# New order of projection tiles and new lane paces in a fused mLSTM + S5 decoder block

## The chip, the cores and the metric

The kernel runs on one core of a Trainium2 chip. The metric is the device time of one execution in microseconds, the median of several. The core has a matrix engine (PE in the profile, its weight loads PEld), a vector engine (DVE), a scalar engine (ACT), GpSimd (POOL) and a queue engine that here only issues transfers (SP). Each works through its own list of instructions; semaphores tie them together.

## What is computed

One decoder block over 16 meta and 1024 real positions, width 1024, all in float32:

```
p     = h @ w_in + b_in            columns [u_s5 | q | k | v | o | i | f | g_s5 | g_m]
y_s5  = GLU(GELU(S5(u_s5)))        S5: diagonal complex recurrence, 32 groups of 16
y_m   = (o * HeadNorm(mLSTM(q, k, v, i, f))) @ m_w_out     4 heads, chunkwise
mix   = sigmoid(g_s5) * y_s5 + sigmoid(g_m) * y_m
h     = LN(alpha * h + mix @ w_o)
h     = LN(alpha * h + relu(h @ w_up + b_up)^2 @ w_down)
```

q and k pass a causal convolution of width 4 and a SiLU first. GLU(z) is the first half of `z @ w_glu` times the sigmoid of the second.

## The kernel before

**Arithmetic.** Each float32 operand of a large product is split into a high part (a copy to float32r by ACT, `whi`, `hT_hi`, `gelh`) and the remainder (a subtraction by DVE, `wlo`, `hT_lo`, `gell`). A product is three matmuls, lines 226 to 228 in `mm3`. So each weight tile costs one transfer (SP, line 198, tile `wraw`), one ACT copy (line 212) and one DVE subtraction (line 213) before PE can use it. `split_w` gives the split a higher scheduling priority; a job's weights are split while the job ahead of it runs, and loaded while the one or two ahead of that run.

**Jobs.** After the first layer norm (`ln0_pipe`, up to about 75 us) the projections run as a list of jobs, in the order of the string `ORDER`. A `q` entry makes two jobs, q and k of a head. `v` jobs make the values of a head, `u` jobs the inputs of S5, `o` jobs the output gate of half a head, `g` jobs the S5 gate (8 tiles), `m` jobs two of the 8 tiles of the gate g_m. Behind them come eight GLU jobs, z0 to z7, then the rest of g_m and the output product (`first`, `run7`, with sums of weights formed by POOL transfers in `w_sums`), then the output projection and the feed-forward part.

**Lanes.** The recurrences are generators in queues called lanes. `ml` holds the gate computation and the four heads of the mLSTM one after another, `cv` the convolutions, `s5c` the tables and constants of S5, `s5` its four batches, `s5g` the GELU, `ah` the scaling of the residual and the early preparation of up-projection weights (`up_early`). After every two terms of a product `mm3` calls `pump`, which adds the planned time of these matmuls to a clock and lets each lane take its next step if its last `yield` is over:

```
def pump(dt):
    clock[0] += dt
    for l in lanes.values():
        l.run(clock[0])
```

With 512 columns dt is 1.28. A step is emitted at the first such call after it is due. The numbers in the lists `ML`, `NL`, `C5`, `K5`, `D5`, `W5`, `Y5` are the yields, by head or by S5 batch. A head of `mlstm` first loads its decay rows from DRAM, forms them by DVE and ACT (lines 440 to 452; yields 6.0, nine of 0.3, 4.0), and then walks over 9 chunks with two yields of ML[h] each, with a norm of four chunks (`N`) after chunk 5 and at the end. Then the two tiles of the head are ready for its `o` jobs.

Two places don't pace. Ahead of an `o` job the `ml` lane is stepped at once until its head is ready, and at z0 the S5 lanes are drained. What is emitted is then ordered for each engine by the framework's scheduler, with the order of emission as priority.

**Memory.** 30 slots of 128 x 1056 floats (`big`) hold weights, lanes, S5 tiles, gates and GELU outputs. Before, the 8 S5 gate tiles `SG` and the 8 GELU tiles `GEL` (high and low of 4 batches) stay in slots from where they are made until the GLU jobs use them; z_f takes `SG[f]` over as `MIX[f]`.

**Queues.** SP issues nearly all transfers: weights, the S5 round trips through DRAM (us_dr, cs_dr, ct_dr, ys_dr), hm_dr (line 913, an o job's result), act_dr. POOL issues w_sums (line 995) and the small transfers of S5's constants.

Of the kernel before, what the change touches and what calls it, by code (L numbers as in the profile page):

```python
# [9 lines left out]
F32 = mybir.dt.float32  # L10
F32R = mybir.dt.float32r
# [26 lines left out]
LN2_1 = 0.693359375  # L38
LN2_2 = math.log(2.0) - LN2_1
MAGIC = 1.5 * 2 ** 23  # L40
ORDER = "q0 q1 v0 q2 v1 q3 o1 o0 v2 o2 o3 u0 u1 v3 u2 g0 u3 g1 o4 o5 o7 o6 g2 g3 g5 g6 g4 g7 m0 m1"
S5_START = "v0"
NM = 2
SPLIT_UP = 200
PRE = 3
ZD = 1
ML = [2.4, 1.2, 1.68, 4.8]
NL = [0.88, 1.75, 1.75, 1.75]
C5 = [1.9, 1.9, 1.9, 1.9]
K5 = [1.7, 1.7, 1.7, 1.7]  # L50
Z5 = [1.0, 1.0, 1.0, 1.0]
D5 = [2.88, 1.22, 1.44, 1.44]
W5 = [2.21, 1.56, 2.6, 2.6]
Y5 = [1.97, 2.82, 3.38, 2.82]
AFT = 0
VAFT = 2
LOAD0 = "x0 x1 w0 c0 x2 w1 c1 x3 x4 w2 x5 w3 x6"
# [55 lines left out]
def decoder_block(  # L113
# [4 lines left out]
    nc = tc.nc  # L118
    v_, a_, g_, t_ = nc.vector, nc.scalar, nc.gpsimd, nc.tensor
# [9 lines left out]
    def slot(name, dt=F32):  # L129
        return big.tile([P, SLOT], dt, tag="s", name=name)  # L130
# [7 lines left out]
    def f32(ap):  # L138
        return ap.bitcast(F32)
# [1 line left out]
    def row_bcast(src, n, off=0):  # L141
        return bass.AP(tensor=src.tensor, offset=src.offset + off, ap=[[0, P], [1, n]])

    lanes = {"ml": Lane(), "cv": Lane(), "s5": Lane(), "s5c": Lane(), "s5g": Lane(), "ah": Lane()}
    clock = [0.0]

    def pump(dt):
# [131 lines left out]
    QK, VT, HM, HMREADY = {}, {}, {}, set()  # L279
# [31 lines left out]
    def v_job(h):  # L311
        W = 264 if h == 0 else 256
        if h == 0:
            loads = [(wv0[:, 4 * i:4 * i + 4].rearrange("p k f -> p (k f)"), 4 * W) for i in range(2)]
        else:
            loads = [(wv[h - 1, :, 4 * i:4 * i + 4].rearrange("p k f -> p (k f)"), 4 * W) for i in range(2)]

        def run(job):
            bvt = mid.tile([P, DV], F32, tag="bvt", bufs=1, name="bvt")
            nc.sync.dma_start(bvt, row_bcast(bv, DV, h * DV))  # L320
            if h == 0:
                v_.memset(IF[:, 0, 0, :], NEG)
                v_.memset(IF[:, 1, 0, :], 100.0)
            v0 = mid.tile([P, 258], F32, tag="v0", bufs=2, name="v0")
            v12 = [slot("v12"), slot("v12")]
            vt = [v0] + [v12[i // 4][:, (i % 4) * 258:(i % 4) * 258 + 258] for i in range(8)]
            VT[h] = vt
            for i in range(NCH):
                c0, n = chunk(i)
                ps = mmps()  # L330
                terms = []
                for k in range(KT):
                    wh, wl = job.w[k // 4]
                    s = slice((k % 4) * W, (k % 4) * W + W)
                    terms.append((hT_hi[:, k, c0:c0 + n], hT_lo[:, k, c0:c0 + n], wh[:, s], wl[:, s]))
                g_.memset(vt[i][:n, DV:DV + 1], 1.0)
                if i == 0:
                    for k in range(KT):
                        _, _, wh, wl = terms[k]
                        t_.matmul(ps[:48, :W], meta_hl[:, k, :], wh, start=(k == 0), stop=(k == KT - 1))  # L340
                    p2 = mmps()
                    for k in range(KT):
                        _, _, wh, wl = terms[k]
                        t_.matmul(p2[:n, :W], meta_hl[:, k, :n], wl, start=(k == 0), stop=(k == KT - 1))
# [13 lines left out]
                if i == VAFT:
                    job.after()
            if h == 0:  # L360
                lanes["ml"].add(gates())
            lanes["ml"].add(mlstm(h))
        all_jobs.append(Job(loads, run))

# [64 lines left out]
                          bass.AP(tensor=src.tensor, offset=src.offset + (4 + h) * P,  # L429
                                  ap=[[0, P], [4 * P, NCH - 1], [1, P]]))  # L430

    def mlstm(h):
        while (h, 1) not in QK:
            yield 0.5
        qT, kT, vt = QK[h, 0], QK[h, 1], VT[h]
        gB, wiB = slot("gB"), slot("wiB")
        bcast_row(gB, grow_dr, h)
        bcast_row(wiB, wrow_dr, h)
# [232 lines left out]
    GEL = {}  # L671
# [4 lines left out]
    def s5_tables():  # L676
        lo, hi, tmp = ([slot("s5T"), slot("s5T")] for _ in range(3))
        c1, s1 = (t[:, :1040].rearrange("p (q c) -> p q c", q=16) for t in lo)
        c2, s2 = (t[:, :1040].rearrange("p (q c) -> p q c", q=16) for t in hi)
        g_.memset(c1[:, :, 0], 1.0)  # L680
        g_.memset(s1[:, :, 0], 0.0)
        g_.tensor_copy(c1[:, :, 1], S5["p8"][:, 0])
        g_.tensor_copy(s1[:, :, 1], S5["p8"][:, 1])
        yield 1.9

        def product(oc, os, n, m, ac, as_, bc, bs):
            w1, w2 = (t[:, 0:16 * m].rearrange("p (q c) -> p q c", q=16) for t in tmp)
            sh = [P, 16, m]
            cmul(v_, oc, os, ac, as_, bc.to_broadcast(sh), bs.to_broadcast(sh), w1, w2)
        n = 1  # L690
        while n < 64:
            product(c1[:, :, n + 1:2 * n + 1], s1[:, :, n + 1:2 * n + 1], n, n, c1[:, :, 1:n + 1], s1[:, :, 1:n + 1],
                    c1[:, :, n:n + 1], s1[:, :, n:n + 1])
            n *= 2
            yield 1.9
        product(c2[:, :, 0:64], s2[:, :, 0:64], 64, 64, c1[:, :, 1:65], s1[:, :, 1:65], c1[:, :, 64:65], s1[:, :, 64:65])
        yield 3.8
        product(c2[:, :, 64:65], s2[:, :, 64:65], 128, 1, c1[:, :, 1:2], s1[:, :, 1:2], c2[:, :, 63:64], s2[:, :, 63:64])
        for r in range(2):
# [187 lines left out]
    def s5_gelu(b):  # L887
        yield 3.0
        yc = slot("s5yc")
        for g in range(8):  # L890
            src = ys_dr[b, :, (g % 2) * 4 + g // 2, :].rearrange("(t h) c -> h t c", h=16)
            nc.sync.dma_start(yc[16 * g:16 * g + 16, 0:1024].rearrange("p (t c) -> p t c", t=8), src)
        yield 14.0
        gf = slot("gelf")
        a_.activation(gf[:, 0:1024].rearrange("p (c t) -> p t c", t=8),
                      yc[:, 0:1024].rearrange("p (t c) -> p t c", t=8), AF.Gelu_apprx_tanh)
        hi, lo = slot("gelh", F32R), slot("gell", F32R)
        a_.activation(hi[:, 0:1024], gf[:, 0:1024], AF.Copy)
# [21 lines left out]
        return hi, lo  # L920

    MIX, SG, SGM = {}, {}, {}

    def gs_job(f):
        def evac(bi, c0, c1, ps):
            if bi == 0:
                SG[f] = slot("sgs")
            a_.activation(SG[f][:, c0:c1], ps, AF.Sigmoid, bias=bft[:, JGS + f:JGS + f + 1])
        fm_job(JGS + f, HALF, META, evac)

    def glu_job(f):
        def run(job):
# [560 lines left out]
    for i, j in enumerate(jobs):  # L1493
# [612 lines left out]
```

## Time and profile before

| | us |
|---|---|
| median of 3 runs | 1594.03 (1590.19 to 1595.22) |
| the profiled execution | 1587.66 |
| its span, from the first to the last instruction | 1585.9 |
| mean granted PE clock | 0.981 |

The stages, by the profile: the first norm with the first projections until 75 us; projections, mLSTM, S5 and GLU until about 720 us, with gates and output product behind; feed-forward from about 980 us on. In the views below, a waits row reads "engine line waited for: total, times, longest"; a row of a timeline reads "start, length, engine, line, operation, tiles, shape, [idle before, and what ended it]"; a row of lines reads "line, engine, operation, tiles, count | busy, mean ns | idle before"; a row of transfers reads "tiles, queue, count, KB each, us to landing".

### The profile page before, as it was taken

The page shows a single profiled execution, that of the slowest core. Times are in us where ns is not written, and L with a number is a line of the kernel's source. Part 1 is how long each engine was busy: PE and PEld are TensorE (multiplying, and loading weights), DVE is VectorE, ACT ScalarE, POOL GpSimd, SP SyncE. Part 2 cuts the span into 40 slices and gives each one's busy share as a digit, 9 for nine tenths or more (in the row PEclk, how much of TensorE's full clock was granted, in tenths as well). Part 3 has the DMA queues.
Part 4 walks back from the last instruction along what each step waited for, and adds up shares of the span by engine and source line. Part 5 has one row for each costly group of instructions (what it writes and reads, how often), then busy time and mean ns, then how long its engine had stood idle before and what let it go on. Part 6 is the DMA issues. An engine that isn't in the chain of part 4 may idle for free.

```text
span 1585.9 us, 20447 instructions
## 1 busy us (share of the span) xinstructions
PE 1521.4 (96%) x7593; PEld 1282.3 (81%) x7593; DVE 1059.3 (67%) x1939; ACT 642.0 (40%) x982; POOL 93.5 (6%) x183
## 2 busy tenths in 40 slices
PE   7998989999897999999999999999999999999997
PEld 7997969899776878777788888888888888888886
DVE  7797766445556234468779666766666769775876
ACT  5623444533344231235545224544444534432440
POOL 0010413200000011000000001000000000000000
PEclk9998999999998999999999999999999999999999
DMA  8527433464562565677335226744444699666642
GB/s 297 166 48 119 125 98 119 148 181 152 159 157 71 140 197 197 219 280 255 128 126 180 81 80 208 256 140 151 148 154 145 198 362 336 233 219 237 227 171 107
DMA packets 150308, 278.15 MB, mean 175 GB/s; under 512 B 39472, under 2 KB 61688, under 8 KB 150152
## 3 DMA queue, kind: packets, MB, share of 16 engines
q1 hardware_dynamic: 124144, 249.84, 47.1%
q0 software_dynamic: 26064, 27.01, 7.1%
q8 instruction: 59, 0.97, 0.2%
q14 instruction: 41, 0.34, 0.1%
HBM read 197.21 MB, written 92.97 MB: 183 GB/s over the span
## 4 chain that ended last, share of the span: by engine, by line
PE 39%; issue 15%; DMA 1%; DVE 0%; SPq 0%; ACT 0%; POOLq 0%
PE mm L228 9%; PE mm L227 9%; PE mm L226 9%; PE sd L226 3%; PE sd L227 3%; PE sd L228 3%; DMA rawb<-h_dr 1%; PE ln L1593 0%; DMA wraw<-in_wf_dram 0%; DVE wlo L1064 0%; DVE rawb L1023 0%; SPq L1045 0%; POOLq L2102 0%; ACT whi L1063 0%; ACT hT_hi L1018 0%
## 5 line engine op out<-in xcount | busy, mean ns | idle before, releaser
L226 PE MATMUL mm<-hT_hi,whi 128*128 128x512 f32 (+3 forms) x604 | 228.1, 378 | 3.7 <-ACT whi L212 3.7
L228 PE MATMUL mm<-hT_hi,wlo 128*128 128x512 f32 (+3 forms) x604 | 226.9, 380 | 4.1 <-DVE wlo L1064 2.9
L227 PE MATMUL mm<-hT_lo,whi 128*128 128x512 f32 (+3 forms) x604 | 228.7, 379 | 0.0
L228 PEld LDWEIGHTS mm<-hT_hi,wlo 128*128 128x128 f32 x604 | 115.1, 191 | 24.7 <-DVE wlo L1064 3.8
L226 PEld LDWEIGHTS mm<-hT_hi,whi 128*128 128x128 f32 x604 | 115.0, 190 | 21.9 <-ACT whi L212 4.2
L227 PEld LDWEIGHTS mm<-hT_lo,whi 128*128 128x128 f32 x604 | 114.9, 190 | 18.3 <-issue 0.3
L227 PE MATMUL sd<-dwl,dah 128*128 128x512 f32 x240 | 94.4, 393 | 0.0
L228 PE MATMUL sd<-dwh,dal 128*128 128x512 f32 x240 | 94.2, 393 | 0.0
L226 PE MATMUL sd<-dwh,dah 128*128 128x512 f32 x240 | 94.1, 393 | 0.0
L1805 ACT ACTIVATE dwh<-wdr 128x1024 fp32r<-128x1024 f32 x56 | 58.9, 1054 | 85.7 <-DMA wdr<-in_wdn_dram 24.1
L1801 ACT ACTIVATE dah<-da 128x1024 fp32r<-128x1024 f32 x56 | 58.6, 1052 | 84.1 <-PE sd L227 34.7
L213 DVE TENSOR_TENSOR wlo<-wraw,whi 128x1024 fp32r<-128x1024 f32 (+1 forms) x46 | 56.1, 1222 | 54.6 <-ACT whi L212 51.5
L227 PE MATMUL mm<-dwl,dah 128*128 128x512 f32 (+1 forms) x224 | 84.5, 378 | 0.0
L226 PE MATMUL mm<-dwh,dah 128*128 128x512 f32 (+1 forms) x224 | 84.5, 378 | 0.0
L228 PE MATMUL mm<-dwh,dal 128*128 128x512 f32 (+1 forms) x224 | 84.5, 378 | 0.0
L1802 DVE TENSOR_TENSOR dal<-da,dah 128x1024 fp32r<-128x1024 f32 x56 | 68.1, 1219 | 22.3 <-ACT dah L1801 22.2
L1806 DVE TENSOR_TENSOR dwl<-wdr,dwh 128x1024 fp32r<-128x1024 f32 x56 | 68.2, 1219 | 12.7 <-ACT dwh L1805 12.1
L226 PE MATMUL mm<-whi,hT_hi 128*128 128x256 f32 (+1 forms) x256 | 75.6, 295 | 0.9 <-DVE mlo L348 0.9
L227 PE MATMUL mm<-wlo,hT_hi 128*128 128x256 f32 (+1 forms) x256 | 75.2, 294 | 0.0
L228 PE MATMUL mm<-whi,hT_lo 128*128 128x256 f32 (+1 forms) x256 | 74.5, 291 | 0.0
L228 PE MATMUL mm<-th,wul 128*128 128x512 f32 x156 | 61.6, 395 | 0.0
L227 PE MATMUL mm<-tl,wuh 128*128 128x512 f32 x156 | 61.4, 394 | 0.0
(473 smaller groups left out, 3675.1 us busy)
## 6 DMA issues: line engine op xcount, KB each, us to landing
da<-act_dr SPq DMA_DIRECT2D x56, 512.0 KB, 5.2
wdr<-in_wdn_dram SPq DMA_DIRECT2D x56, 512.0 KB, 6.5
wur<-in_wup_dram SPq DMA_DIRECT2D x32, 512.0 KB, 4.3
act_dr<-upy SPq DMA_DIRECT2D x64, 256.0 KB, 2.6
wraw<-in_wf_dram SPq DMA_DIRECT2D x30, 512.0 KB, 7.2
wu_dr<-wpre SPq DMA_DIRECT2D x21, 512.0 KB, 5.3
wpre<-wu_dr POOLq DMA_DIRECT2D x21, 512.0 KB, 5.0
act_dr<-upx SPq DMA_DIRECT2D x32, 256.0 KB, 4.0
```

What stands on the lines that cost most here:

```text
L213: todo.append(lambda e=v_, r=r, hi=hi, lo=lo, n=n: e.tensor_tensor(lo[:, :n], r[:, :n], f32(hi[:, :n]), op=OP.subtract))
L226: t_.matmul(ps, ah, bh, start=(i == 0 and part[0]), stop=False, skip_group_check=skip)
L227: t_.matmul(ps, ah, bl, start=False, stop=False, skip_group_check=skip)
L228: t_.matmul(ps, al, bh, start=False, stop=(i == n - 1 and part[1]), skip_group_check=skip)
L1801: a_.activation(ah[:, :D], a[:, :D], AF.Copy)
L1802: v_.tensor_tensor(alo[:, :D], a[:, :D], f32(ah[:, :D]), op=OP.subtract)
L1805: a_.activation(wh, raw[i], AF.Copy)
L1806: v_.tensor_tensor(wl, raw[i], f32(wh), op=OP.subtract)
```

## The change

The order of jobs and all paces are replaced:

```diff
-ORDER = "q0 q1 v0 q2 v1 q3 o1 o0 v2 o2 o3 u0 u1 v3 u2 g0 u3 g1 o4 o5 o7 o6 g2 g3 g5 g6 g4 g7 m0 m1"
+ORDER = "q0 q1 v0 g0 v1 q2 g1 g2 v2 g3 o0 o1 u0 u1 q3 o2 o3 u2 v3 u3 o4 o5 g4 g5 g6 m0 g7 o6 o7 m1"
+GEL_BACK = "m1"
-ML = [2.4, 1.2, 1.68, 4.8]
-NL = [0.88, 1.75, 1.75, 1.75]
-C5 = [1.9, 1.9, 1.9, 1.9]
-K5 = [1.7, 1.7, 1.7, 1.7]
+ML = [2.0, 2.0, 2.0, 2.0]
+NL = [2.5, 2.5, 2.5, 2.5]
+C5 = [3.0, 3.0, 3.0, 3.0]
+K5 = [3.0, 3.0, 3.0, 3.0]
-D5 = [2.88, 1.22, 1.44, 1.44]
-W5 = [2.21, 1.56, 2.6, 2.6]
-Y5 = [1.97, 2.82, 3.38, 2.82]
+D5 = [5.0, 5.0, 5.0, 5.0]
+W5 = [1.5, 1.5, 1.5, 1.5]
+Y5 = [2.0, 2.0, 2.0, 2.0]
```

The decay rows of a head become a generator of their own in a new lane `mp`, which takes the gate computation too. The rows of head h are formed once head h - 1 has begun its chunks:

```diff
             if h == 0:
-                lanes["ml"].add(gates())
+                lanes["mp"].add(gates())
+            lanes["mp"].add(decay(h))
             lanes["ml"].add(mlstm(h))
...
-    def mlstm(h):
-        while (h, 1) not in QK:
+    def decay(h):
+        while (h, 1) not in QK or (h and h - 1 not in HEAD_ON):
             yield 0.5
...
         yield 4.0
+        PR[h] = gB, qi, dec
...
+    def mlstm(h):
+        while h not in PR:
+            yield 0.5
+        HEAD_ON.add(h)
...
             while int(j.tag[1:]) not in HMREADY:
                 lanes["cv"].drain()
+                lanes["mp"].drain()
                 lanes["ml"].step()
```

The GELU tiles of batches 0 and 1 are stored to DRAM and loaded again ahead of m1 by POOL; all S5 gate tiles are stored by their g job and loaded two GLU jobs ahead of their use:

```diff
-        GEL[b] = (hi, lo)
+        if b < 2:
+            for i, t in enumerate((hi, lo)):
+                nc.sync.dma_start(gl_dr[b, i], f32(t[:, :D]))
+        else:
+            GEL[b] = (hi, lo)
...
+    def sg_load(f):
+        if f < KT:
+            MIX[f] = slot("mix")
+            nc.sync.dma_start(MIX[f][:, :D], sg_dr[f])
+
+    def gel_load(b):
+        GEL[b] = (slot("gelh", F32R), slot("gell", F32R))
+        for i in range(2):
+            g_.dma_start(GEL[b][i][:, :D], gl_dr[b, i])
...
+            if bi == 1:
+                nc.sync.dma_start(sg_dr[f], SG.pop(f)[:, :D])
...
-            MIX[f] = SG.pop(f)
+            sg_load(f + 2)
...
+        if j.tag == GEL_BACK:
+            gel_load(0)
+            gel_load(1)
+            sg_load(0)
+            sg_load(1)
```

`product` in the S5 tables loses an argument that it never used. The `ah` lane still starts at g4, which now stands earlier in the order.

More of the change, by code (lines that the diff above doesn't have):

```diff
@@ L142, in row_bcast @@
         return bass.AP(tensor=src.tensor, offset=src.offset + off, ap=[[0, P], [1, n]])
-    lanes = {"ml": Lane(), "cv": Lane(), "s5": Lane(), "s5c": Lane(), "s5g": Lane(), "ah": Lane()}
+    lanes = {"mp": Lane(), "ml": Lane(), "cv": Lane(), "s5": Lane(), "s5c": Lane(), "s5g": Lane(), "ah": Lane()}
     clock = [0.0]
@@ L430, in bcast_row @@
                                   ap=[[0, P], [4 * P, NCH - 1], [1, P]]))
-    def mlstm(h):
-        while (h, 1) not in QK:
+    PR = {}
+    def decay(h):
+        while (h, 1) not in QK or (h and h - 1 not in HEAD_ON):
             yield 0.5
-        qT, kT, vt = QK[h, 0], QK[h, 1], VT[h]
+        qT = QK[h, 0]
         gB, wiB = slot("gB"), slot("wiB")
@@ L451, in mlstm @@
         yield 4.0
+        PR[h] = gB, qi, dec
+    HEAD_ON = set()
+    def mlstm(h):
+        while h not in PR:
+            yield 0.5
+        HEAD_ON.add(h)
+        kT, qT, vt = QK[h, 1], QK[h, 0], VT[h]
+        gB, qi, dec = PR.pop(h)
         kws, sws, Cs = {}, {}, {}
@@ L684, in s5_tables, with product @@
         yield 1.9
-        def product(oc, os, n, m, ac, as_, bc, bs):
+        def product(oc, os, m, ac, as_, bc, bs):
             w1, w2 = (t[:, 0:16 * m].rearrange("p (q c) -> p q c", q=16) for t in tmp)
@@ L691, in s5_tables @@
         while n < 64:
-            product(c1[:, :, n + 1:2 * n + 1], s1[:, :, n + 1:2 * n + 1], n, n, c1[:, :, 1:n + 1], s1[:, :, 1:n + 1],
+            product(c1[:, :, n + 1:2 * n + 1], s1[:, :, n + 1:2 * n + 1], n, c1[:, :, 1:n + 1], s1[:, :, 1:n + 1],
                     c1[:, :, n:n + 1], s1[:, :, n:n + 1])
@@ L695, in s5_tables @@
             yield 1.9
-        product(c2[:, :, 0:64], s2[:, :, 0:64], 64, 64, c1[:, :, 1:65], s1[:, :, 1:65], c1[:, :, 64:65], s1[:, :, 64:65])
+        product(c2[:, :, 0:64], s2[:, :, 0:64], 64, c1[:, :, 1:65], s1[:, :, 1:65], c1[:, :, 64:65], s1[:, :, 64:65])
         yield 3.8
-        product(c2[:, :, 64:65], s2[:, :, 64:65], 128, 1, c1[:, :, 1:2], s1[:, :, 1:2], c2[:, :, 63:64], s2[:, :, 63:64])
+        product(c2[:, :, 64:65], s2[:, :, 64:65], 1, c1[:, :, 1:2], s1[:, :, 1:2], c2[:, :, 63:64], s2[:, :, 63:64])
         for r in range(2):
@@ L922, in decoder_block @@
     MIX, SG, SGM = {}, {}, {}
+    sg_dr = dram.tile([KT, P, D], F32, name="sg_dr")
+    gl_dr = dram.tile([2, 2, P, D], F32, name="gl_dr")
+    def sg_load(f):
[6 more added lines that the diff above has]
+            g_.dma_start(GEL[b][i][:, :D], gl_dr[b, i])
     def gs_job(f):
```

## The prediction

> **What bounds the kernel now.** I read the page's busy line first, then one row for each of three stages.
>
> ```profile
> PE 1521.4 (96%) x7593; PEld 1282.3 (81%) x7593; DVE 1059.3 (67%) x1939; ACT 642.0 (40%) x982; POOL 93.5 (6%) x183
> ```
> ```profile
> 0.00:75.00 75.00, 65.26 (x512) 63.14 (x513) 55.12 (x186) 45.88 (x75) 4.25 (x17) 0.95 0.67 237
> 75.00:745.00 670.00, 624.22 (x3410) 540.30 (x3409) 399.09 (x865) 251.66 (x390) 76.87 (x144) 0.96 0.53 154
> 745.00:1585.90 840.90, 831.94 (x3675) 678.89 (x3673) 605.07 (x889) 344.42 (x518) 12.37 (x22) 1.00 0.55 187
> ```
> A row gives length, busy time of PE, PEld, DVE, ACT and POOL, granted PE clock, DMA share and GB/s. PE is the bound. The change touches nothing before 75 us or behind 745 us, so all is decided in the middle row. There PE idles 670.0 - 624.2 = 45.8 us, and loses more at a lowered clock. The change adds and removes no matmul, so **idle time and lowered clock are all that it can win**. The same view cut finer shows where they lie:
>
> ```profile
> 125.00:150.00 25.00, 19.69 (x133) 17.75 (x132) 18.86 (x45) 9.07 (x16) 0.51 (x5) 0.80 0.55 94
> ...
> 200.00:252.00 52.00, 45.13 (x245) 37.77 (x244) 36.37 (x93) 27.54 (x44) 13.66 (x28) 0.93 0.43 118
> ...
> 285.00:300.00 15.00, 12.91 (x70) 10.16 (x69) 7.41 (x23) 11.49 (x17) 5.06 (x10) 1.00 0.80 237
> ...
> 430.00:450.00 20.00, 13.58 (x62) 10.52 (x61) 11.96 (x30) 7.43 (x16) 2.52 (x2) 0.91 0.63 152
> ...
> 470.00:520.00 50.00, 39.44 (x173) 30.92 (x171) 31.46 (x88) 19.27 (x32) 2.87 (x2) 0.90 0.34 101
> ...
> 555.00:580.00 25.00, 21.23 (x80) 16.30 (x79) 8.56 (x8) 11.29 (x11) 4.85 (x4) 0.86 0.61 203
> ...
> 660.00:700.00 40.00, 35.99 (x145) 27.71 (x144) 24.55 (x38) 14.68 (x24) 0.00 (x0) 0.96 0.73 263
> ...
> 720.00:745.00 25.00, 22.10 (x84) 17.40 (x83) 21.43 (x21) 14.32 (x17) 0.00 (x0) 0.86 0.54 184
> ```
> Idle is length minus PE; clock loss is length times (1 - clock). In order, idle + clock: **A** 5.3 + 5.0, **B** 6.9 + 3.6, **C** 2.1 + 0, **E** 6.4 + 1.8, **F** 10.6 + 5.0, **G** 3.8 + 3.5, **H** 4.0 + 1.6, **I** 2.9 + 3.5. That is 42.0 + 24.0 = 66.0 us; the other 3.8 us of idle time are crumbs elsewhere, which I leave. What ended the gaps stands in the waits of PE (total, times, longest), in the same stage:
>
> ```profile
> PE pt L513 <- DVE hraw L506: 7.2, 2, 4.2
> PE mm L226 <- ACT whi L212: 6.7, 3, 3.7
> PE s5z L823 <- DMA s5yc<-ys_dr: 4.3, 1, 4.3
> PE mm L344 <- DVE wlo L213: 3.6, 2, 3.4
> PE pu L477 <- DVE sw L465: 3.0, 2, 2.5
> PE mm L228 <- DVE wlo L1064: 2.9, 1, 2.9
> PE mm L228 <- DVE wlo L213: 2.2, 5, 0.9
> ```
> L513, L477: recurrence steps of the mLSTM heads (B, C, F). L226 waiting for whi: a late projection weight (G, H). s5z: S5's constants (E). L344: weights of v1 (A). L1064: the first weights of the gate products behind z7 (I).
>
> **Pacing (B, C, F).** `pump` adds to a planned clock what the emitted matmuls should take: 10.2 to 10.4 planned us for an o, g, u, q or k job, 22.5 for a v job. A lane's next step is emitted once its yields are due. These are orders, not times. Adding them up by hand from the start of v0, in planned us: before, o1 stands at 87 (v0 22.8, q2 and k2 20.8, v1 22.5, q3 and k3 20.8), while head 0 starts its chunks at 57, and 18 steps of ML = 2.4 need over 43. So chunks 5 to 8 and both norms of head 0 are emitted in one piece ahead of o1; likewise chunks 6 to 8 of head 1 ahead of o2 (B, C), and at o7 (planned 256) chunks 3 to 8 of head 3, whose 18 steps of 4.8 need 86 and got 33 (F). Such a piece is a chain from DVE to ACT to PE with little beside it: that is the wait for hraw.
>
> After: every head gets 18 steps of 2.0, taken at pumps of 1.28, so 46, with its norms 65 to 69. Heads end at 122, 191, 256 and 321; o0, o2, o4 and o6 stand at 130, 192, 256 and 327. Only at o4 is something still forced: the last norm of head 2 and the decay rows of head 3, as v3 is only one job ahead. Gain: B 10.5 + C 2.1 + F without the 1.7 us that s5z waits in it, 13.9 = **26.5 us**. What is late next is o4. Row for row its chain is:
>
> ```profile
> gB<-grow_dr SPq DMA_DIRECT2D x4, 512.0 KB, 7.1
> ```
> ```profile
> L444 DVE SCALAR_TENSOR_TENSOR gB<-gB,acol,mask 128x128 f32<-128x128 f32 (+1 forms) x36 | 10.1, 332 | 18.5 <-DMA gB<-grow_dr 18.5
> ...
> L448 ACT ACTIVATE gB<-gB 128x1024 f32<-128x1024 f32 x4 | 4.2, 1060 | 9.7 <-DVE gB L444 9.7
> ```
> 7.1 + 9 x 0.33 + 1.1 = 11 us, against 4 planned us until head 3's first update. Matmuls of o4 and o5 fill in unless PE's order puts the update ahead of them: 0 to 7 us, I take **3**, as no wait of PE in the profile names gB. The lane itself adds no work: the DVE and ACT rows above are the same 36 and 4.
>
> **The clock** is below 1.00 only in stretches that hold a gap over 2 us. [...] The longest gap of F:
>
> ```profile
> 501.98 0.66 PE L513 MATMUL pt<-ident,hraw 128*128 128x128 f32 x2 [2.96 <-DVE hraw L506]
> ```
> [...]
>
> **SP's queue (G).** An SP store that waits holds all weight loads issued behind it:
>
> ```profile
> SPq L913 <- DVE hmF L910: 47.6, 2, 44.5
> ```
> That is hm_dr of o7, held by F's forced head; the weights of g6 came late. After, o6 and o7 follow a finished head, so G goes: **7.3 us**. The change adds 20 SP issues: 8 stores and 8 loads of sg_dr, 4 stores of gl_dr. A store of sg_dr waits for the second ACT evacuation of its own job, then the weights two jobs ahead go; a late one is a late weight. An issue takes SP little:
>
> ```profile
> 423.55 0.38 SPq L813 DMA_DIRECT2D s5Mi<-cs_dr  x1
> ```
> 20 x 0.38 = 8 us, spread over more than 300, is hidden while SP has idle time. Moved bytes: 24 x 0.5 = 12.6 MB on 103 MB, 0.53 to 0.59 DMA share. No ACT or DVE instruction is added; the sigmoids of g0 to g3 move to where ACT is idle half of the time.
>
> **Slots (H, I).** 30 slots hold weights, lanes and S5. At z0 to z4 before, 8 gate tiles, 8 of GEL, 2 gates and 6 weights leave few for up_early, whose stores then hold SP:
>
> ```profile
> SPq L1437 <- DVE wpre L1436: 50.5, 17, 12.3
> SPq L1045 <- DVE wlo L1064: 5.6, 1, 5.6
> ```
> After, gate tiles leave for DRAM and come back two jobs ahead, and ah and up_early start at planned 276 instead of 317 and end at z1 instead of z5. So nothing of up_early is left before the loads behind z7: I goes, **6.4 us**; H moves to z0 and z1, where there is more room: **4** of 5.6.
>
> **Start (A).** DVE is full from 75 to 125 us:
>
> ```profile
> 75.00:125.00 50.00, 50.00 (x369) 49.64 (x367) 47.68 (x109) 11.63 (x14) 6.28 (x18) 1.00 0.37 64
> ```
> ```profile
> 127.67 1.21 DVE L213 TENSOR_TENSOR wlo<-wraw,whi 128x1024 fp32r<-128x1024 f32 x1
> ```
> After, v1 follows g0 instead of q2 and k2, so PE wants its weights about 11 us earlier (near 113), and they are also split one job earlier, at planned 23 instead of 33. If their place in DVE's queue moves along, A vanishes (+10.3); if it stays at 127.7, behind the S5 tables, the wait grows by 11. I take half: **5**, as C5 at 3.0 takes S5 constants out of this stretch.
>
> **E** stays: the loads of S5's constants are issued and wanted at the same step as before (bounds: its own 8.2 us less or more, as 24 transfers are added).
>
> **Reload (z0).** GEL 0 and 1 come back by POOL during m1; the row of such a load is `5.0` to landing:
>
> ```profile
> wpre<-wu_dr POOLq DMA_DIRECT2D x21, 512.0 KB, 5.0
> ```
> ```profile
> 611.32 0.59 POOL L995 DMA_DIRECT2D ws_dr<-ws_dr  x1 [15.08 <-DMA ws_dr<-in_wmo_dram]
> ```
> ```profile
> 557.92 0.39 PE L227 MATMUL mm<-hT_lo,whi 128*128 128x512 f32 x1
> 558.15 0.40 PE L228 MATMUL mm<-hT_hi,wlo 128*128 128x512 f32 x1
> ```
> m1 is 48 matmuls, 0.23 us apart: 11 us. Four loads fit into it, if POOL isn't inside such a wait for its own weight sums: 0 to 15 us, I take **3**, since the program puts the reload first; behind it on POOL stands only the next weight sum, wanted after z7. **Crowding**: decay rows of the next head (3 slots) and slower S5 constants (6) are held longer; by count 32 tiles want 30 slots near planned 66 and 130. I charge **4** for late weights, and **5** for crumbs that a new order makes.
>
> **Sum**: 26.5 + 7.3 + 6.4 + 4 + 5 = 49.2 won; 3 + 3 + 4 + 5 = 15 paid; -34. The profiled execution took 1587.7 us (span 1585.9), so 1553.5; the median of the runs lies 6.4 higher, 1594.0, which makes **1560 us**.
>
> **Rivals.**
> 1. *Half of it* (0.22): gaps move rather than go, with o4, POOL's wait and v1 all at their dear ends: 7 + 15 + 11 paid and A not won. 26.5 + 17.7 - 33 - 9 = 2 won at worst; midway to 34 some 18: 1576.
> 2. *Slower by slots* (0.15): lanes that hold tiles longer leave weight loads without a slot. Price: a late weight costs what G does, 7.3 us. Of some 30 jobs, 5 late ones eat the 34, 8 give 1594 + 8 x 7.3 - 34 = 1618. It decides from the sixth late weight on. For it: the count of 32; against: the old order was as full near o1 and had two.
> 3. *No change* (0.10): the scheduler reorders what is emitted, so the gaps come back in like size elsewhere: 1594. For it: o1 is emitted behind the whole of head 0, yet its matmuls run before the transposes of head 0's last norm:
>
> ```profile
> 204.94 0.39 PE L226 MATMUL mm<-hT_hi,whi 128*128 128x512 f32 x1
> ...
> 234.98 0.66 PE L513 MATMUL pt<-ident,hraw 128*128 128x128 f32 x2 [4.22 <-DVE hraw L506]
> ```
> Against: it didn't prevent B, C and F.
> 4. *Nearly all gaps go* (0.08): crumbs alone remain, 1594 - 62 = 1532.
>
> **Chances.** My forecast has 0.45, from 1546 to 1572. Half of it still is faster. Faster by over 0.3% (what a measurement here can tell from no change, 5 us): 0.45 + 0.22 + 0.08 = 0.75; within: 0.10; slower: 0.15. For 8 in 10 the range leaves out the far ends of rivals 2 and 4: 1538 to 1604.
>
> **What would show it.** Right: in 200 to 520 us no wait for hraw over 1 us and clock 1.00; SP's wait for hmF at L913 under 10 us; no wait of PE for wlo L1064. Wrong: waits of PE for whi L212 at many jobs (rival 2); idle time at z0 ended by gelh or gell (reload); a gap over 10 us at v1's L344 (start); the middle stage's idle time still near 46 us (rival 3).

## The result, and the profile after

The changed kernel took 1641.82 us (median; 1641.34 to 1646.62), the kernel before 1593.27 us beside it (1590.19 to 1595.22). The ratio is 1.0313, with a 95% interval of 1.0288 to 1.0339: **slower by 48 us**, where 1560 had been forecast and 1604 was the upper end of the range.

The same two views as before, the page's busy line and the windows by stage (length, busy time of PE, PEld, DVE, ACT and POOL, granted PE clock, DMA share, GB/s), with the middle stage ending at 800 instead of 745:

```profile
span 1639.5 us, 20498 instructions
...
PE 1529.5 (93%) x7593; PEld 1292.0 (79%) x7593; DVE 1060.9 (65%) x1939; ACT 639.8 (39%) x980; POOL 94.8 (6%) x187
```
```profile
0.00:75.00 75.00, 65.27 (x512) 63.17 (x513) 55.04 (x186) 45.84 (x75) 4.16 (x17) 0.95 0.69 244
75.00:800.00 725.00, 633.82 (x3417) 552.12 (x3417) 400.96 (x866) 249.97 (x389) 78.31 (x148) 0.92 0.54 160
800.00:1639.50 839.50, 830.43 (x3667) 676.73 (x3666) 604.86 (x887) 344.00 (x518) 12.31 (x22) 1.00 0.55 186
```

The number of matmuls is the same, and so are the first and the last stage. The middle one, with 3417 matmuls against 3410, went from 670 to 725 us. Its idle time of PE doubled, 725.0 - 633.8 = 91.2 us against 45.8, and the clock fell from 0.96 to 0.92, which shows as 9.6 us more busy time; 45.4 + 9.6 = 55 us between the two profiled executions, whose spans differ by 53.6; the medians differ by 48. So the place was forecast rightly and the sign wrongly. The waits of PE in that stage (total, times, longest) say that the old gaps went and larger ones came:

```profile
PE s5z L837 <- DMA s5Mi<-cs_dr: 12.2, 2, 10.0
PE pt L527 <- ACT s5Z L847: 11.7, 1, 11.7
PE mm L227 <- DVE z2s L997: 10.8, 1, 10.8
PE mm L227 <- ACT whi L213: 10.6, 1, 10.6
PE mm L227 <- DMA gelh<-gl_dr: 9.1, 1, 9.1
PE mm L229 <- DVE wlo L214: 8.6, 3, 4.3
PE pS L477 <- DVE C L496: 8.6, 1, 8.6
PE pk L472 <- DVE C L496: 4.6, 1, 4.6
PE gps L394 <- DVE gts L391: 4.6, 1, 4.6
```

No wait for hraw in a head is among them: B, C and F are gone. Most of these rows have one large entry and a different releaser each, and the releaser in a row is not the cause but the last to come. The 10.6 us behind whi and the 10.8 behind z2s, followed back in the timeline of the changed kernel (start, length, engine, instruction, idle before and what ended it):

```profile
644.25 0.80 PE L227 MATMUL mm<-hT_hi,whi 128*128 128x512 f32 x1 [10.60 <-ACT whi L213]
...
634.60 0.63 ACT L1467 ACTIVATE wpre<-wur 128x512 fp32r<-128x512 f32 x1 [16.93 <-DMA wur<-in_wup_dram]
...
643.15 1.04 ACT L213 ACTIVATE whi<-wraw 128x1024 fp32r<-128x1024 f32 x1
...
637.37 0.69 DVE L1449 TENSOR_TENSOR wus<-wur 128x512 f32<-128x512 f32 x1 [23.95 <-DMA wur<-in_wup_dram]
...
639.91 0.68 DVE L928 TENSOR_TENSOR hmF<-hmF,osig 128x512 f32<-128x512 f32 x1
...
618.01 0.35 SPq L1459 DMA_DIRECT2D wur<-in_wup_dram  x1
...
623.16 0.33 SPq L199 DMA_DIRECT2D wraw<-in_wf_dram  x1
...
602.99 1.90 POOL L1027 DMA_DIRECT2D ws_dr<-in_wmo_dram  x1 [0.57 <-issue]
...
692.29 0.69 DVE L1449 TENSOR_TENSOR wus<-wur 128x512 f32<-128x512 f32 x1 [18.98 <-DMA wur<-in_wup_dram]
...
694.83 0.68 DVE L997 TENSOR_TENSOR z2s<-mm,z2s 128x512 f32<-128x512 f32 x1
...
695.57 0.80 PE L227 MATMUL mm<-gelh,whi 128*128 128x512 f32 x1 [10.80 <-DVE z2s L997]
```

Two things are late here. The first is a load: m1's weights left SP at 623.2 and landed at 640.0 (16.8 us, in the next fence), so that the copy `whi`, at 643.15, came late even without what stood ahead of it on ACT. The second is an engine that works in order: ACT stood 16.9 us and DVE 24 us at `wur`, the load of a step of `up_early` that nobody needs for 300 us. On ACT this cost the copy at most the 3 us after 640.0, as ACT worked again from 634.6 on; on DVE it held the first `hmF` product until 639.9. At z1 it is plainer: DVE stood 19 us at `wur` with `z2s` behind it, and PE stood 10.8 us at `z2s`. The first `wur` load was issued at 618.0. Transfers from 618 to 638 us: the busy share of the 16 DMA engines in tenths and the GB/s, in 40 slices of 0.5 us, and three loads and stores of that stretch (count, KB each, median us to landing):

```profile
DMA  7397999898999899533222222312222222222222
GB/s 263 61 204 251 346 198 173 196 328 299 340 315 250 228 308 292 165 80 65 72 74 74 78 74 74 98 61 61 66 70 74 78 70 74 74 78 82 86 107 107
...
wur<-in_wup_dram SPq DMA_DIRECT2D x2, 512.0 KB, 17.1
sg_dr<-sgs SPq DMA_DIRECT2D x1, 512.0 KB, 17.3
wraw<-in_wf_dram SPq DMA_DIRECT2D x1, 512.0 KB, 16.8
```

From 627 us on the DMA share is only 0.27, at 77 GB/s (by the windows of 627 to 638 us), and yet everything pending needs 17 us. Of the transfers under way then, one had been issued at 603: a weight sum of `w_sums` (line 1027). The packet records of 627 to 638 us show four to six packets in flight at a time, and half of the busy share is that of POOL's queue, half that of SP's. The sums have their 3 (wf) or 4 (wmo) tiles outermost. The share was 0.27 here beside a sum of 4 tiles, and 0.23 while a sum of 3 tiles ran alone in the kernel before (508 to 531 us); of 16 engines that is the work of 4.3 and of 3.7. The author's estimate from these numbers is that a sum keeps about as many engines busy as it has tiles. The same sums in both kernels, over the whole trace:

```profile
ws_dr<-in_wmo_dram POOLq DMA_DIRECT2D x6, 1024.0 KB, 28.8
ws_dr<-in_wf_dram POOLq DMA_DIRECT2D x6, 768.0 KB, 27.7
```
```profile
ws_dr<-in_wmo_dram POOLq DMA_DIRECT2D x6, 1024.0 KB, 31.5
ws_dr<-in_wf_dram POOLq DMA_DIRECT2D x6, 768.0 KB, 28.2
```

They are as slow before (the first fence) as after. Each row mixes two plain copies with four transfers that add: single ones, in both kernels, took 12 to 22 us (copies) and 25 to 40 us (adding). So the theory became, with that estimate: a sum leaves 3 or 4 DMA engines with long work for some 30 us; any load issued meanwhile has a part on these engines and lands late; the change places loads that DVE, ACT or PE wait for into such stretches more often.

The trace's records of semaphores fit it. They hold sixteen marks for each transfer named here, and its landing in the views is the last of them. A sum's own marks fall apart: of the sum of 4 tiles issued at 603.0 in the changed kernel, twelve came within 8.7 us and four after 33.8 to 34.7 us; of the one of 3 tiles issued at 323.4, thirteen came within 6.0 us and three after 30.8 to 31.1 us. So do those of other transfers beside a sum. For m1's weights, issued at 623.2 beside a sum of 4 tiles, twelve marks came within 4.4 us and the last four after 15.7 to 16.8 us; for the weights issued at 344.0 beside a sum of 3 tiles, thirteen came within 3.6 us and the last three after 15.6 to 15.8 us. Of SP's transfers in the middle stage whose landing the trace tells (184 before, 200 after), 20 took over 12 us before and 46 after. In 18 of the 20 and 43 of the 46 the last 3 or 4 marks, as many as a transfer of `w_sums` under way has tiles, came some 4 us or more behind the others. The `wur` loads of `up_early` in the middle stage, before and after:

```profile
wur<-in_wup_dram SPq DMA_DIRECT2D x6, 512.0 KB, 8.0
```
```profile
wur<-in_wup_dram SPq DMA_DIRECT2D x6, 512.0 KB, 16.4
```

### The profile page after: what moved, and what is told of

Read it like the earlier page. It is cut to its first block, busy times and chain, and to the rows that moved or that the text cites. A ratio compares the mean times of both kernels' runs of the same rounds, so it can differ in the third digit from the quotient of the medians.

```text
span 1639.5 us, 20498 instructions
## 1 busy us (share of the span) xinstructions
PE 1529.5 (93%) x7593; PEld 1292.0 (79%) x7593; DVE 1060.9 (65%) x1939; ACT 639.8 (39%) x980; POOL 94.8 (6%) x187
## 3 DMA queue, kind: packets, MB, share of 16 engines
q1 hardware_dynamic: 127024, 260.33, 47.8%
## 4 chain that ended last, share of the span: by engine, by line
PE 59%; issue 16%; DMA 14%; DVE 6%; ACT 3%; SPq 1%; POOL 0%; POOLq 0%; ACTq 0%; DVEq 0%
PE mm L229 15%; PE mm L227 15%; PE mm L228 15%; PE sd L228 3%; PE sd L227 3%; PE sd L229 3%; DMA ws_dr<-in_wf_dram 2%; DMA wur<-in_wup_dram 2%; DMA s5Mi<-cs_dr 2%; DMA gB<-grow_dr 1%; DMA wu_dr<-wpre 1%; DMA x<-in_x_dram 1%; DMA s5U<-us_dr 1%; DMA mix<-sg_dr 1%; PE mm L1360 1%
## 5 line engine op out<-in xcount | busy, mean ns | idle before, releaser
L227 PE MATMUL mm<-hT_hi,whi 128*128 128x512 f32 (+3 forms) x604 | 236.6, 392 | 10.6 <-ACT whi L213 10.6
L229 PE MATMUL mm<-hT_hi,wlo 128*128 128x512 f32 (+3 forms) x604 | 233.6, 390 | 9.0 <-DVE wlo L214 8.6
L228 PE MATMUL mm<-hT_lo,whi 128*128 128x512 f32 (+3 forms) x604 | 235.3, 390 | 0.0
L229 PEld LDWEIGHTS mm<-hT_hi,wlo 128*128 128x128 f32 x604 | 119.0, 197 | 29.8 <-DVE wlo L214 10.0
L227 PEld LDWEIGHTS mm<-hT_hi,whi 128*128 128x128 f32 x604 | 119.4, 198 | 29.4 <-ACT whi L213 11.0
L228 PEld LDWEIGHTS mm<-hT_lo,whi 128*128 128x128 f32 x604 | 119.2, 197 | 18.0
L1840 DVE TENSOR_TENSOR dal<-da,dah 128x1024 fp32r<-128x1024 f32 x56 | 68.1, 1219 | 23.2 <-ACT dah L1839 22.5
L1844 DVE TENSOR_TENSOR dwl<-wdr,dwh 128x1024 fp32r<-128x1024 f32 x56 | 68.2, 1219 | 12.1 <-ACT dwh L1843 11.6
L214 DVE TENSOR_TENSOR wlo<-wraw,whi 128x1024 fp32r<-128x1024 f32 (+1 forms) x46 | 56.1, 1221 | 30.3 <-ACT whi L213 21.3
L227 PE MATMUL mm<-gelh,whi 128*128 128x512 f32 x128 | 51.6, 412 | 19.9 <-DVE z2s L997 10.8
L1449 DVE TENSOR_TENSOR wus<-wur 128x512 f32<-128x512 f32 x16 | 11.1, 691 | 82.1 <-DMA wur<-in_wup_dram 58.3
```

Of the source, the lines that this page charges most:

```text
L214: todo.append(lambda e=v_, r=r, hi=hi, lo=lo, n=n: e.tensor_tensor(lo[:, :n], r[:, :n], f32(hi[:, :n]), op=OP.subtract))
L227: t_.matmul(ps, ah, bh, start=(i == 0 and part[0]), stop=False, skip_group_check=skip)
L228: t_.matmul(ps, ah, bl, start=False, stop=False, skip_group_check=skip)
L229: t_.matmul(ps, al, bh, start=False, stop=(i == n - 1 and part[1]), skip_group_check=skip)
L1449: v_.tensor_tensor(n1[:, 0:512], a21, a22, op=OP.add)
L1840: v_.tensor_tensor(alo[:, :D], a[:, :D], f32(ah[:, :D]), op=OP.subtract)
```

## The experiments

Times are medians; each ratio is to the kernel before, run on the same chip beside it, with its 95% interval. The medians of the kernel before lie between 1590.2 and 1593.4 us on the chips used, so a difference of medians from two chips is good to some 3 us.

### Parts of the change, taken away or done alone

**Without the DRAM ways**: S5 gates and GELU tiles stay in slots.

```diff
...
-                nc.sync.dma_start(sg_dr[f], SG.pop(f)[:, :D])
...
-            sg_load(f + 2)
+            MIX[f] = SG.pop(f)
...
-            gel_load(0)
-            gel_load(1)
...
```

> The changed kernel, with the two GELU tiles and the gate tiles kept in their slots as before (no gl_dr, no sg_dr). Theory 'transfers' (the added 12.6 MB crowd the DMA engines): back to about 1595 us, gaps at m1, z0 and z1 (32 us idle in the changed kernel) gone. Theory 'early preparation' (up_early now runs into o6, o7 and m1, and DVE and ACT wait in order for its loads): the gap ended by gelh<-gl_dr goes (11 us and its clock, some 15), the other two at m1 and z1 stay: about 1625 us. Theory 'plan' (order and paces): the middle keeps its 24 us: not under 1615 us.

1632.45 us, 1.0256 [1.0230, 1.0281]. The DRAM ways cost 9 of the 48 us. The gap behind gelh is gone, but DVE still waits 51.6 us for wur, longest 24.1, as against 58.3 in the changed kernel.

**`up_early` later**: the `ah` lane starts at o6 instead of g4, in the changed kernel.

```diff
-        if j.tag == "g4":
+        if j.tag == "o6":
```

> The changed kernel, with the lane of ah_scale and up_early started at o6 instead of g4 (planned 327 instead of 276). 'Early preparation': DVE no longer waits for wur ahead of m1, the 10.6 us gap at m1 goes, z0 and z1 shrink: 1610 to 1620 us. 'Transfers': the reload meets the same traffic, z0 keeps its gap: 1635 us. 'Plan': no change in the middle, under 5 us in all.

1618.74 us, 1.0157 [1.0132, 1.0182]: the early start costs 23 us. The wur loads land after 7.4 us here, and DVE waits 15.3 us for them.

**v3 a job earlier**, so that head 3's decay rows are not forced at o4:

```diff
-ORDER = "... u2 v3 u3 o4 ..."
+ORDER = "... v3 u2 u3 o4 ..."
```

> The changed kernel, with v3 ahead of u2 (v3 u2 u3 o4 instead of u2 v3 u3 o4), so that the decay rows of head 3 are asked for one job earlier and less is forced at o4. If the forced rows at o4 make the 11.7 us gap near 490 us (DVE and ACT wait 12 us for gB ahead of the norm of head 2): that gap falls under 4 us and the time by 10 to 18 us, to some 1628 us. If the gap is S5's (s5Z), no change: 1640 us.

1652.43 us, 1.0373 [1.0341, 1.0405], so 11 us slower. Between 450 and 560 us the wait of 11.7 us at o4 went and one of 14.4 for `s5yc<-ys_dr` came. So taking the forced decay chain away there doesn't pay by itself.

**The old order and paces** in the changed kernel; lane and DRAM ways stay.

```diff
-ORDER = "q0 q1 v0 g0 v1 q2 g1 g2 v2 g3 ..."
+ORDER = "q0 q1 v0 q2 v1 q3 o1 o0 v2 o2 ..."
...
-ML = [2.0, 2.0, 2.0, 2.0]
+ML = [2.4, 1.2, 1.68, 4.8]
```

(and the other pace lists alike)

> The changed kernel with the order and all paces of before: the decay lane and both ways through DRAM stay. 'Plan': about the time of before, 1590 to 1600 us. 'Transfers': they cost here too, 1615 to 1640 us. 'Early preparation': as up_early starts late again, 1590 to 1605 us, but the reload at z0 may cost up to 10.

1640.86 us, 1.0296 [1.0272, 1.0320]. The same loss comes without the new order, with other gaps: 20.5 us behind gelh, 11.2 for hraw, 8.9 for C.

The next three have one part each in the kernel before. Order and paces only, the decay rows within the head's own lane (`yield from decay(h)`):

> Before, with nothing but the new order and paces (gates and decay rows in the ml lane, nothing through DRAM). If the plan itself costs the time: 1625 to 1640 us, as the same with the decay lane took 1632. If the decay lane is what hurts (DVE and ACT waiting in order for its row loads): 1600 to 1615 us. If the plan is right and only misses its lane and its slots: it forces heads at o0, o2 and o6 again and is slower than 1632.

1657.87 us, 1.0416 [1.0398, 1.0433]. The decay lane only:

> Before, with nothing but the decay lane. Theory 'any move': each part shifts where in-order waits for loads fall, with no part to blame: 1595 to 1615 us. Theory 'lane': row loads ahead of their use cost 10 us or more with any order: above 1603 us. Theory 'harmless lane': 1588 to 1598 us.

1606.44 us, 1.0093 [1.0078, 1.0108]. The DRAM ways only:

> Before, with nothing but the ways through DRAM. In the run with lane and DRAM on the old order, z0 waited 20.5 us for gelh<-gl_dr. If the reload behind POOL's weight sums is the cost of this part: that gap is here too, and the time is 1615 to 1630 us. If the gap came from the lane: 1593 to 1603 us.

1619.13 us, 1.0175 [1.0160, 1.0190]. **Each part alone is slower**, +67, +16 and +29 us, and the three together, +48, are better than the sum, 112. So no single part is the culprit. (The run with order and paces has the early start in it too, as g4 stands earlier.) In the last one a single wait of PE holds most of the loss, 21.9 us for gelh; its load was issued on POOL behind a copy of one sum into the next, which had waited 28.4 us. The row names a store of ah_dr, but the copy reads what an adding transfer wrote, and that one, issued at 586.8, landed at 633.2, 46.4 us later:

```profile
633.49 0.60 POOL L1024 DMA_DIRECT2D ws_dr<-ws_dr  x1 [28.42 <-DMA ah_dr<-ahr]
634.14 0.59 POOL L949 DMA_DIRECT2D gelh<-gl_dr  x1
```

**Late start and no DRAM ways together**, with the new plan and the lane:

> The changed kernel with ah_scale and up_early started at o6 and nothing through DRAM. If the two late costs (early preparation 23 us, DRAM 9 us) add: 1608 to 1613 us, the rest being the middle. If up_early needs the slots that the DRAM ways free: above 1619 us.

1602.12 us, 1.0067 [1.0052, 1.0082]. Order, paces and lane still cost 9 us. From here the early start costs 1632.45 - 1602.12 = 30 us and the DRAM ways another 9.

**Is it POOL's place?** The DRAM ways only, with the reload issued by SP:

```diff
-            g_.dma_start(GEL[b][i][:, :D], gl_dr[b, i])
+            nc.sync.dma_start(f32(GEL[b][i][:, :D]), gl_dr[b, i])
```

> The order and paces of before with the ways through DRAM and no decay lane (1619 us), with the two GELU tiles loaded back by SP instead of POOL. POOL stood 28 us at a weight sum right ahead of these loads. If the place behind that sum is the cost: the 22 us gap ended by gelh<-gl_dr falls under 5 us and the time to 1588 to 1598 us. If the DMA engines are simply full there (every load of that stretch took 13 to 22 us): the gap stays over 12 us and the time over 1607 us.

1619.32 us, 1.0171 [1.0147, 1.0196]: nothing won. SP stood behind stores of `ah_dr` and `sg_dr` and issued the loads at 630.8, only 3 us earlier than POOL had; PE waited 12.3 us for gelh and 4.2 for gell. So the run doesn't tell what an early issue would be worth; it shows that this change of queue moves the load from one late place to another.

**Is it the waiting in order?** The kernel without DRAM ways, with 16 planned us between a wur load and its use:

```diff
                 nc.sync.dma_start(r[j][:, :D], wup[2 * p + j].rearrange("p k f -> p (k f)"))
-            yield 3.0
+            yield 16.0
```

> New order, paces and decay lane, nothing through DRAM (1632 us), with up_early still started at g4 but its step after the loads of wur set from 3.0 to 16.0 planned us. If the cost of the early start is that ACT and DVE wait in order for wur (20 and 58 us of waits in the changed kernel): the waits at m1, z0 and z1 go and the time falls to 1600 to 1612 us. If it is slots or traffic of the early work: 1625 us or more.

1608.00 us, 1.0117 [1.0088, 1.0147]: 24 us won, with no wait of DVE for wur left. So of the early start's 30 us, most goes with DVE and ACT standing at a load. (The longer yield also puts each step 13 planned us later, which this run doesn't tell apart.)

**Does a gap's removal pay in the old order?** The kernel before, with o7 and o6 moved behind g6 and head 3 paced at 2.0:

```diff
-ORDER = "... o4 o5 o7 o6 g2 g3 g5 g6 g4 g7 m0 m1"
+ORDER = "... o4 o5 g2 g3 g5 g6 o7 o6 g4 g7 m0 m1"
-ML = [2.4, 1.2, 1.68, 4.8]
+ML = [2.4, 1.2, 1.68, 2.0]
```

> Before, with o7 and o6 moved behind g6 (o4 o5 g2 g3 g5 g6 o7 o6 g4 g7 m0 m1) and ML of head 3 from 4.8 to 2.0, so that head 3 is out before o7 asks for it; nothing else. If pacing takes the stall F away as I forecast, with the late weights G that hang on it: some 15 to 20 us less, 1572 to 1580 us. If gaps of that size come back elsewhere: 1588 to 1600 us. If the longer held slots cost: above 1600 us.

1591.14 us, 0.9993 [0.9981, 1.0005]. Gaps F and G, 13.9 + 7.3 in the forecast, are gone, and the time is the same: PE waits 6.1 for z2s, 4.1 for sgm and 3.6 for wlo between 560 and 690 us instead.

### The weight sums

**Half of the sums left out**: the transfers that add (8 of 16) are not issued, once in the kernel of 1602 us and once in the kernel before, so both lack that part of the sums in the g_m tiles from 2 on and in the output product.

```diff
-            tc.keep_in_program_order(g_.dma_start(d, a, accum_op=OP.add) if add else g_.dma_start(d, a))
+            if not add:
+                tc.keep_in_program_order(g_.dma_start(d, a))
```

> The changed kernel with the late start of up_early and nothing through DRAM (1602 us), without the adding half of the weight sums on POOL (8 of 16 transfers left out, so the g_m tiles from 2 on and the output product of the mixers come out wrong). If POOL and the DMA engines, held by these sums, make the middle gaps (8.6 us near 216, s5z waits, z0): these gaps go and the time falls by 15 us or more, to 1587 or less. If not: under 5 us of change.

1563.23 us, 0.9826 [0.9807, 0.9845].

> The kernel before without the adding half of the weight sums (8 of 16 transfers left out; g_m tiles from 2 on and the output product come out wrong). The late start without DRAM fell by 39 us from the same cut. If the sums are what sets the new order back: before falls by under 20 us. If they slow every order alike: by 30 to 40 us.

1573.84 us, 0.9882 [0.9865, 0.9900]. The new plan gains 39 us from it and the old one 19, for the same transfers left out. With them the plan and the lane lose 9 us to the kernel before; without, they win 11.

**The same sums, laid wide**: all sums are made, with the 128 rows outermost instead of the 3 or 4 tiles.

```diff
-ap=[[2 * KT * P * P, n0], [KT * P, P], [1, 512]]
+ap=[[KT * P, P], [2 * KT * P * P, n0], [1, 512]]
...
-d = [ws_dr[p0:p0 + n0, i] for i in range(4)]
+d = [ws_dr[p0:p0 + n0, i].rearrange("n p f -> p n f") for i in range(4)]
```

In the changed kernel, otherwise whole:

> The changed kernel with the weight sums on POOL laid out with the 128 rows outermost instead of the 3 or 4 tiles; the same bytes, the same results. In the trace a sum keeps only 3 to 4 packets in flight for some 30 us, and loads issued meanwhile land 15 to 24 us later. If that tail is what the moved loads (wur, gl_dr, S5's constants, rows of decay) run into: the sums take under 12 us, the gaps near 348, 644, 668 and 696 us shrink, and the time falls by 30 us or more, to 1612 or less. If the loads are late for other traffic: within 10 us of 1642.

1572.27 us, 0.9872 [0.9855, 0.9889]. In the kernel before:

> The kernel before with the same new layout of the weight sums and nothing else. If the tail is the cost and the old order only met it less: a gain too, but smaller than in the changed kernel, 5 to 20 us (1572 to 1587). If the old order was fitted to the sums as they were: 1588 to 1600 us.

1565.48 us, 0.9834 [0.9813, 0.9855]. **One layout is worth 70 us to the changed kernel and 28 to the one before.** The transfers of the first of the two:

```profile
ws_dr<-in_wmo_dram POOLq DMA_DIRECT2D x6, 1024.0 KB, 11.5
ws_dr<-in_wf_dram POOLq DMA_DIRECT2D x6, 768.0 KB, 8.8
...
wur<-in_wup_dram SPq DMA_DIRECT2D x6, 512.0 KB, 8.3
...
gelh<-gl_dr POOLq DMA_DIRECT2D x2, 512.0 KB, 14.3
```

The sums land in 9 to 12 us instead of 28 to 32 (medians), and the wur loads, of which nothing was changed, in 8.3 instead of 16.4. In neither wide kernel do the last marks of a late transfer stand apart: of 14 and 5 transfers of SP that took over 12 us in the middle stage, none has a step of over 2 us between two marks. With wide sums the change still costs 1572.27 - 1565.48 = 7 us. Three more kernels, all wide, say which part. New plan and lane, no DRAM ways, late start:

> The changed kernel with the late start of up_early, nothing through DRAM (1602 us), and the new layout of the sums. If the tail is the cost: 1565 to 1580 us, as with half of the sums left out (1563), and faster than before. If the layout doesn't matter: 1597 to 1605 us.

1543.83 us, 0.9699 [0.9677, 0.9721], the best of all and below both ranges. The same with the DRAM ways, so the whole change but for the late start:

> The changed kernel, whole, with the new layout of the sums and up_early started at o6 instead of g4. It tells what the ways through DRAM cost once the tail is gone, beside 1544 us without them. If the reload at z0 still waits: 1555 to 1565. If the ways are free by themselves: 1540 to 1548.

1549.55 us, 0.9735 [0.9712, 0.9758]. No DRAM ways, early start:

> New order, paces and decay lane, new layout of the sums, nothing through DRAM, up_early from g4 on as in the changed kernel. Beside 1544 us with the late start and 1572 us for the changed kernel with the layout. If the early start of up_early costs by itself (waits for wur without a tail): 1560 to 1575. If it only cost because of the tail: 1540 to 1550.

1562.91 us, 0.9819 [0.9798, 0.9839].

The steps from the kernel before to the changed one, in us, with narrow and with wide sums (differences of the medians above):

| step | narrow | wide |
|---|---|---|
| kernel before | 1593.3 | 1565.5 |
| new order, paces and lane | +8.9 | -21.7 |
| `up_early` from g4 on | +30.3 | +19.1 |
| S5 gates and GELU via DRAM | +9.4 | +9.4 |
| changed kernel | 1641.8 | 1572.3 |

The layout of the sums makes 42 of the 48 us: in this order of steps 31 of them by turning the plan's gain of 22 into a loss of 9, and 11 at the early start. What is left is a gain of 22 and two costs of 19 and 9. The sizes depend on the order: with the late start the DRAM ways cost 16.6 us narrow (1618.74 - 1602.12) and 5.7 wide (1549.55 - 1543.83).

The best kernel's middle stage, by windows and by the waits of PE:

```profile
75.00:703.00 628.00, 614.17 (x3439) 538.80 (x3439) 406.28 (x870) 251.11 (x391) 66.44 (x144) 0.99 0.58 167
```
```profile
PE gps L394 <- DVE gts L391: 4.6, 1, 4.6
PE mm L229 <- DVE wlo L1090: 2.9, 2, 2.0
PE s5p L777 <- DVE ecol L424: 2.2, 1, 2.2
```

13.8 us of idle time are left of 45.8, and the clock is 0.99. Of the gaps B to I only I's weights are left, 2.9 us in two pieces, without loss of clock.

The early start's cost with wide sums, too, is seen at DVE's waits for wur. With the early start (no DRAM ways, wide), then with the late one:

```profile
DVE wus L1443 <- DMA wur<-in_wup_dram: 32.2, 3, 13.0
```
```profile
DVE wus L1443 <- DMA wur<-in_wup_dram: 6.0, 2, 4.7
```

With the early start the loads themselves land in 7.3 us (median), but they leave late: DVE's longest wait began at 597.0, SP issued the two loads at 601.0 and 602.4, behind seven stores of `wu_dr`, and they landed at 608.0 and 610.0.

## Why the prediction was wrong, step by step

**What bounds it** held: all 55 us between the profiled executions lie in the middle stage, in idle time and clock.

**Pacing (B, C, F; 26.5)**: the mechanism held, its pay didn't. In 200 to 520 us of the changed kernel the one wait over 1 us that an hraw ended is 2.5 us, of S5's product for ACT; none is in a head. But gaps of 8.6, 10.0 and 11.7 us came into the same stretch, and its clock is 0.94 instead of the 1.00 that was to show success. The first, at 218.6, shows in the waits from 200 to 222:

```profile
POOL s5Mx L802 <- DMA ws_dr<-in_wf_dram: 20.3, 1, 20.3
...
DVE s5tm L756 <- DMA s5Mx<-s5Kt: 9.9, 1, 9.9
...
PE pS L477 <- DVE C L496: 8.6, 1, 8.6
```

POOL stood 20.3 us at a sum, an S5 transfer behind it on POOL went late, DVE stood 9.9 us for the slot that this transfer frees, and the state C of a head came late. Order, paces and lane win their 22 us only where the sums are wide (11 with half of the sums left out).

**The failed step** is here: the sum takes landing times as fixed numbers from rows of the old order (7.1 us for gB, 5.0 for a reload) and prices the new order by them. In the changed kernel head 3's decay row gB landed after 23.6 us and the four reloads after 18 to 25. The row of the sums, 28.8 us, stood in the same view; I weighed it only as a wait of POOL, never as something beside which other loads land late. In the changed kernel 46 of SP's transfers took over 12 us, against 20 before (25 with order, paces and lane alone), and order, paces and lane, which were to win, lost 9 us; with wide sums they won 22. The second error is to add gaps up as if each were the last obstacle: 21 us of F and G, taken out of the old order by themselves, gave 1 us, and the interval of that ratio includes no change.

**o4's decay chain (3, bounds 0 to 7)** was mis-sized. The row gB was issued in two parts at 462 and 463, and the second landed at 486.5, beside a sum of 4 tiles: twelve of its sixteen marks came within 6.5 us, the last four after 23.2. DVE and ACT stood at them, and the copies of S5's states for PE stood behind:

```profile
481.08 0.22 DVE L448 SCALAR_TENSOR_TENSOR gB<-gB,acol,mask 16x16 f32<-16x16 f32 x1 [12.10 <-DMA gB<-grow_dr]
...
481.12 1.28 ACT L451 ACT_TABLE_LOAD   x1 [10.28 <-DMA gB<-grow_dr]
...
489.93 0.43 ACT L847 ACTIVATE s5Z<-s5z 64x130 f32<-64x130 f32 x2
```

PE waited 11.7 us for that s5Z. I had said that matmuls of o4 and o5 fill in; they did not. SP, too, was held: its issue of the next row, `wiB`, took 13.0 us at 464.3, against 3.3 before and 2.4 in the changed kernel with wide sums, so the prediction's 0.38 us of an issue is not a fixed price either.

**Slots (H and I, 4 and 6.4)**: I is gone as forecast (no wait of PE worth naming for L1096). For H, the early end of `up_early` was booked as a gain of 4; the early start cost 30 us, with its steps standing at `wur` ahead of z2s and `hmF` on DVE, and to a small part ahead of m1's weights on ACT. I had looked at the slots and at SP, where these steps came from, and not at the two queues that they went into. This term had the wrong sign, and it is the largest part of what is left with wide sums.

**SP's queue (G, 7.3)**: gone at its place, but SP's wait for hmF is 18.2 us in total and 12.1 at most, over the 10 I had set. That one lies ahead of the store at 293.8, where the timeline has `hmF` waiting on DVE for its own job's evacuation by ACT, so it isn't the forced head of before.

**Start (A, 5)** was not won: PE waits 4.6 for gts at 132, 4.3 for wlo at 153 and 3.2 for ecol at 160. The wait moved from v1's weights to the gates, and to q2's weights, whose split stood on DVE behind the decay rows of head 0 (11.2 us for gB). The waits for gts and ecol stay in the best kernel, where 125 to 165 us is the only stretch of the middle stage below full clock.

**E** came out at the bound: 12.2 us for s5Mi instead of 4.3 for s5yc; the load was issued at 333.6, ten us behind a sum. With wide sums and the late start it is gone.

**Reload (3, bounds 0 to 15)** cost 9.1 us behind gelh, within its bounds; the load left POOL at 649.4, behind a copy of one sum into the next. All DRAM ways together cost 9.4 in the table. **Crowding and crumbs (9)** were not tried by themselves.

**The clock**: the length of a gap alone doesn't decide it. In the changed kernel a gap of 2.2 us that ended at 464.7 was followed by half clock (0.50 from 466 to 469 us), and one of 2.5 us that ended at 241.4 by none (1.00 from 238 to 250). The price of the lost clock was too high: length times (1 - clock) counts idle time too. The seven stretches of the middle stage at clock 0.50 add up to 47.8 us, in which PE was busy for 37.0, so they cost 18.5 us and not 24.0; F's 5.0 is 2.9.

**Rivals.** Rival 2 had the sign and 1618 us, at 0.15, by late weights at many jobs. That is not what happened: PE waited long for whi once, and that load was late by its landing. Slots were not tested by themselves. Rival 3's thought, that gaps come back elsewhere, describes the narrow kernels best, but as a rise and not as no change.

**What stays open.** That the sums sit on 3 or 4 of the DMA engines is the author's estimate from packets in flight, busy share and the last 3 or 4 marks; the packet records don't name the engine. The wide layout keeps the bytes and the results, and with it the late marks and 70 us go. A wide sum is also done sooner (medians of 9 to 12 us in the changed kernel, against 28 to 32), so POOL, too, may be held for a shorter time (20.3 us ahead of the gap at 218.6 with narrow sums); how the 70 us split between late landings and POOL's waits, and which load costs how much, is not shown. Why the DRAM ways cost 29 us alone and 9 with the new plan, and 17 with the late start and narrow sums, was not followed up.

## What to carry to other kernels

Before a new order is priced with landing times of the old one, look for transfers that are long at a low DMA share (here 25 to 40 us, at 0.23 to 0.27): beside them loads landed late (m1's weights after 16.8 us), and a slow transfer that costs 28 us in one order can cost 70 in another. Try such a transfer with a longer dimension outermost; here, with 128 rows in place of 3 or 4 tiles, that is two lines, and it was worth more than the whole plan. Put a filler step on an engine that the needed work goes through only when its load has landed (DVE stood 24 and 19 us at `wur`, with `hmF` and `z2s` behind it): give it a due time far behind its load (16 planned us in place of 3 won 24 us), and ask what needed work stands behind it.

## What the runs showed of the hardware

- A transfer of 0.75 or 1 MB from DRAM to DRAM that adds on the way took 25 to 40 us with 3 or 4 tiles outermost (kernels before and after) and 7 to 16 us with 128 rows outermost (the same two, wide), for the same bytes; a plain copy took 12.4 to 22.0 us and 4.5 to 12.4. One that ran alone had a DMA share of 0.23 and 35 GB/s (before, 508 to 531 us), and laid wide 0.81 and 152 GB/s (best kernel, 177 to 183.5 us).
- Of SP's transfers in the middle stage that took over 12 us, 18 of 20 before and 43 of 46 after got the last 3 or 4 of their sixteen semaphore marks, as many as a sum under way has tiles, some 4 us or more behind the others: for m1's weights, 512 KB, twelve within 4.4 us and four after 15.7 us, at a DMA share of 0.27 from 627 us on. So a low DMA share was no sign there that a load would be quick.
- The clock held through a gap of 2.0 us in the best kernel (at 685.9 us; the windows' clock from 675 to 705 is 1.00), and through one of 2.5 us in the changed kernel (at 241.4 us), while it fell to half after one of 2.2 us there (at 464.7 us); F's longest gap of 2.96 us stood in a stretch at 0.90.
